# Decoding the chosen sub-keys and experts of a routed feed-forward layer for four heads at once

## The chip, the cores and the metric

One core of one Trainium2 chip runs one program on inputs that lie in HBM. The metric is the device time in microseconds (us), lower is better. The kernel before took 3133.07 us (median of 3 runs, 3132.15 to 3140.36).

## The reference, cut to what matters

The program is a stack of transformer blocks over 512 tokens of width 1024: two blocks with a dense feed-forward part, then one block whose feed-forward part is a product-key expert layer. The change lies in that layer's routing:

```
q = (x_blk @ w_query).reshape(b, t, PEER_HEADS, 2, HALF_KEY)
scores = jnp.einsum('bthcd,hcnd->bthcn', q, sub_keys)
top_s, top_i = lax.top_k(scores, PEER_TOPK)
cand_s = top_s[..., 0, :, None] + top_s[..., 1, None, :]
cand_i = top_i[..., 0, :, None] * N_KEYS + top_i[..., 1, None, :]
...
best_s, pos = lax.top_k(cand_s, PEER_TOPK)
expert_idx = jnp.take_along_axis(cand_i, pos, axis=-1)
```

There are 8 heads, 128 keys in each half, and 16 kept of each top-k. So each token and head has 16 x 16 candidates, of which 16 positions are kept. A position 0 to 255 says which of the 16 kept keys of the first half (position shifted right by 4) and which of the second half (position and 15) were taken; decoding looks up the numbers of those two keys.

## The kernel before, in words

The work runs on five engines, each with its own queue: TensorE (PE) for products, VectorE (DVE), ScalarE (ACT), GpSimd (POOL), and SyncE (SP), which issues most DMAs. All products are made in three passes over operands that are split in a high and a low part. `split` (line 227) writes the high part on ACT (L228) and the low part on DVE or POOL (L229); `load_w` loads weights of 128x1024 and splits each half so. `LO` says which engine makes the low part: both halves on POOL during the first token half, one on POOL and one on DVE during the second.

The expert layer treats the 512 tokens as two halves of 256 (`PA` and `PB`, two objects of the class `Peer`), each of two tiles of 128 tokens (`NT` = 2). `queries` (line 1429) makes the query of a head with PE, copies it with ACT (L1439), and then calls `route` (line 1449) for the head before. For each of the two tiles `route` scores the keys with PE (L1456), copies the scores to `sc` with ACT (L1459), of which there are two buffers, and then works on DVE alone:

- `top16` (L1465 to L1469) twice over 128 scores and once over the 256 sums `cand` (L1477): five instructions each, max, index, replace, max, index.
- the decode, once per head and tile: `tf` (L1475) turns the key numbers into floats; for each half c, `ai` (L1485) cuts the position, `af` (L1488) turns it into a float, `oh` (L1490) compares it with 0 to 15, `oh` (L1492) multiplies by the key numbers, and a sum along 16 (L1493) writes the number to `i1` or `i2`. For the first tile of the first half (`ng` = 1), two more, `xi` (L1497) and `ix` (L1498), make the number of the expert's row.

So a head and tile have 11 decode instructions, 13 where `xi` and `ix` are made. The 256-wide ones are three in each half.

The generators are woven together by `alongside`: each has a number of steps, and at every turn the one that is least far along goes next. During `PA.queries` the last dense feed-forward part (`ffn_b`) goes along, during `PB.queries` the scores of all experts for three of the four tiles (`scores`, products of 128x384) and the gathered rows of the fourth (`gather_a`: an indirect DMA on POOL, L1503, and one 128x1024 multiply and sum on DVE, L1517). A scheduler then orders the instructions of each engine from this program order and a timing model of its own; every engine runs its queue in order. After `PB.queries` come the one-hot tables (`spread`, L1550 to L1564) and the sums over all experts (`experts`, L1614 to L1670), whose accumulators stay in PSUM throughout; the change has no line there.

Of the kernel before, what the change touches and what calls it, by code (L numbers as in the profile page):

```python
# [9 lines left out]
F = mybir.dt.float32  # L10
FR = mybir.dt.float32r
I32 = mybir.dt.int32
U32 = mybir.dt.uint32
I8 = mybir.dt.int8
AF = mybir.ActivationFunctionType
OP = mybir.AluOpType
AX = mybir.AxisListType
# [35 lines left out]
F_1, F_2, F_3, F_4, L_4 = 1, 36, 2, 20, 1  # L53
L_A = 0.01
S_1, S_2, G_1, G_2, G_3 = 20, 40, 60, 80, 260
# [114 lines left out]
def alongside(main, *others):  # L170

    live = [[g, n, 0] for g, n in (main,) + others]
    while True:
        e = min(live, key=lambda e: e[2] / e[1])
        e[2] += 1
        try:
            next(e[0])
        except StopIteration:
            if e[0] is main[0]:
                return  # L180
            live.remove(e)
# [7 lines left out]
def build(tc, A, out, stop=None, dump=None):  # L189
    nc = tc.nc  # L190
    V, SC, PE, GP = nc.vector, nc.scalar, nc.tensor, nc.gpsimd
    ctx = ExitStack()
    with ctx:
# [8 lines left out]
        def ps(w=S):  # L202
            t = psum.tile([128, S], F, name="ps")
            return t[:, :w] if w < S else t
# [131 lines left out]
        class Norm:  # L336


            def __init__(self, x, gcol, xh, xl, w=S, acc=None, sq=None, R=None):
                self.x, self.g, self.xh, self.xl, self.w = x, gcol, xh, xl, w  # L340
                self.done, self.squared = 0, 0
                self.acc = tmp.tile([128, w], F, name="sqa", bufs=1) if acc is None else acc
                self.r = tmp.tile([128, 4], F, name="rcol", bufs=4)[:, :w // 128]
                self.R = tmp.tile([128, w], F, name="R") if R is None else R
                self.sq = sq
# [204 lines left out]
        with tc.tile_pool(name="l0", bufs=1) as lp:  # L550
# [97 lines left out]
            for g in range(4):  # L648
# [6 lines left out]
                b = 8 + n // 2 - 1  # L655
# [87 lines left out]
        with tc.tile_pool(name="l1", bufs=1) as lp:  # L743
# [24 lines left out]
            p = ps()  # L768
# [186 lines left out]
        ffn_b = ffn1(W)  # L955
# [416 lines left out]
        iota = pe.tile([128, 128], F, name="iota")  # L1372
# [6 lines left out]
        RP = {}  # L1379
# [28 lines left out]
        class Peer:  # L1408
            def __init__(self, h, xh, xl, pool, ng):
                self.xh, self.xl, self.ng = xh, xl, ng  # L1410
                self.q0, self.t0, self.sl = h.q0, h.t0, h.sl
                self.h2 = [hp.tile([128, D], F, name="h2", bufs=ng) for _ in range(ng)]
                self.sd = [pe.tile([128, 8, 16], F, name="sd", bufs=ng) for _ in range(ng)]
                self.ix = [pe.tile([128, 8, 16], I32, name="ix", bufs=ng) for _ in range(ng)]
                self.bs, self.i1, self.i2 = ([pool.tile([128, 8, 16], F, name=n, bufs=2) for _ in range(NT)]
                                             for n in ("bs", "i1", "i2"))
                self.idx = {}

            def rows(self, t):

# [28 lines left out]
            def route(self, hd, qh):  # L1449
                rp = RP[0]  # L1450
                keysT = rp.tile([128, 2, 128], F, name="keysT", bufs=2)
                nc.sync.dma_start(keysT, A["keysT"][:, 2 * hd:2 * hd + 2])
                for t in range(NT):
                    p = ps(W)
                    for c in range(2):
                        PE.matmul(p[:, c * 128:(c + 1) * 128], qh[:, c, t * 128:(t + 1) * 128], keysT[:, c],  # L1456
                                  start=True, stop=True)
                    sc = rp.tile([128, 256], F, name="sc", bufs=2)
                    SC.activation(sc, p, AF.Copy)  # L1459
                    yield  # L1460
                    ts = rp.tile([128, 2, 16], F, name="ts", bufs=2)
                    ti = rp.tile([128, 2, 16], U32, name="ti", bufs=2)

                    def top16(vals, idx, src):
                        V.max(vals[:, 0:8], src)  # L1465
                        V.max_index(idx[:, 0:8], vals[:, 0:8], src)
                        V.match_replace(src, vals[:, 0:8], src, LOWEST)
                        V.max(vals[:, 8:16], src)
                        V.max_index(idx[:, 8:16], vals[:, 8:16], src)  # L1469

                    for c in range(2):
                        top16(ts[:, c], ti[:, c], sc[:, c * 128:(c + 1) * 128])
                        yield
                    tf = rp.tile([128, 2, 16], F, name="tf", bufs=2)
                    V.tensor_copy(tf, ti)  # L1475
                    cand = rp.tile([128, 256], F, name="cand", bufs=2)
                    V.tensor_add(cand.rearrange("p (a b) -> p a b", a=16), ts[:, 0][:, :, None].to_broadcast([128, 16, 16]),  # L1477
                                 ts[:, 1][:, None, :].to_broadcast([128, 16, 16]))
                    bp = rp.tile([128, 16], U32, name="bp", bufs=2)
                    top16(self.bs[t][:, hd], bp, cand)  # L1480
                    yield
                    x = (self.i1[t][:, hd], self.i2[t][:, hd])
                    for c in range(2):
                        ai = rp.tile([128, 16], I32, name="ai", bufs=2)
                        V.tensor_scalar(ai, bp.bitcast(I32), (4, 15)[c], None,  # L1485
                                        op0=(OP.logical_shift_right, OP.bitwise_and)[c])
                        af = rp.tile([128, 16], F, name="af", bufs=2)
                        V.tensor_copy(af, ai)  # L1488
                        oh = rp.tile([128, 16, 16], F, name="oh", bufs=2)
                        V.tensor_tensor(oh, af[:, :, None].to_broadcast([128, 16, 16]),  # L1490
                                        iota[:, None, :16].to_broadcast([128, 16, 16]), op=OP.is_equal)
                        V.tensor_mul(oh, oh, tf[:, c][:, None, :].to_broadcast([128, 16, 16]))  # L1492
                        V.reduce_sum(x[c], oh, axis=AX.X)  # L1493
                        yield
                    if t < self.ng:
                        xi = rp.tile([128, 16], F, name="xi", bufs=2)
                        V.scalar_tensor_tensor(xi, x[0], 128.0, x[1], op0=OP.mult, op1=OP.add)  # L1497
                        V.tensor_copy(self.ix[t][:, hd], xi)  # L1498
                        self.idx[t, hd] = self.ix[t][:, hd]

            def gather(self, table, t, hd, j):
# [197 lines left out]
        PA = Peer(HA, xh, xl, pe, NG)  # L1699
# [7 lines left out]
        gather_a = gathered()  # L1707

        alongside((normed(0, W, xh, xl), 20), (ffn_b, F_3))
        alongside((PA.queries(), 140), (ffn_b, F_4), (gather_a, L_4))  # L1710
        low(LO_Z)
        for _ in ffn_b:
            pass
# [20 lines left out]
        PB = Peer(HB, yh[:, :, rest], yl[:, :, rest], dp, 0)  # L1734
# [13 lines left out]
                    yield from p.one_hots(t)  # L1748

        scores_ = scores(yh, yl)  # L1750
        alongside((PB.queries(), 114), (scores_, S_1), (gather_a, G_1))
        alongside((spread(), 69 * NV), (scores_, S_2), (gather_a, G_2))
        for _ in scores_:
            pass
# [35 lines left out]
```

## Time and profile before

| | us |
|---|---|
| median of 3 runs | 3133.07 |
| the profiled execution, its own time | 3134.13 |
| its span in the trace | 3132.4 |
| outside the span | 1.7 |
| PE busy | 2938.3 (94%) |
| DVE busy | 2207.6 (70%) |
| ACT busy | 1372.6 (44%) |
| POOL busy | 1147.2 (37%) |

Busy time is summed over the whole span. The chain that ended last is 71% PE and 21% DVE. Which engine sets the pace is another one in each stage, so the shares of the whole say little of a change to the routing; the routing of the first token half lies at about 1424 to 1632 us from the start, that of the second at about 1880 to 2164 us.

### The profile page before, as it was taken

The numbers are of one execution on the slowest core, as the hardware profiler recorded it, in microseconds if no ns is written. First come the engines' busy times: TensorE is split into PE (matmuls) and PEld (weight loads), VectorE is DVE, ScalarE is ACT, GpSimd is POOL, SyncE is SP. The second block draws the span as 40 slices with busy tenths as digits, with TensorE's granted clock in tenths as the row PEclk, the third lists the DMA queues.
The fourth block names the chain that finished last, engine by engine and source line by source line (L and its number), as shares of the span: only waits on it lengthen the run. The fifth ranks groups of instructions, "written<-read, shape, count | busy, mean of one in ns | idle before, by whom it ended". The sixth has DMA issues, their size and how long they took to land.

```text
span 3132.4 us, 44864 instructions
## 1 busy us (share of the span) xinstructions
PE 2938.3 (94%) x16770; PEld 2551.2 (81%) x16770; DVE 2207.6 (70%) x4148; ACT 1372.6 (44%) x2347; POOL 1147.2 (37%) x723
## 2 busy tenths in 40 slices
PE   8999999999989889998779989889999999999999
PEld 6468888867689888888769588888999998777787
DVE  6755434477766747658996569999787758888753
ACT  4443222466554545453244543336666653333333
POOL 3110000343320376466554235555554535445200
PEclk9999999999999989999889989999999999999999
DMA  3022232311145533234334038777788779999964
GB/s 132 25 67 101 88 101 88 107 54 48 35 158 194 175 132 125 87 132 142 118 112 151 1 121 281 254 274 256 275 316 305 283 286 383 382 380 370 338 229 151
DMA packets 195883, 568.30 MB, mean 181 GB/s; under 512 B 16944, under 2 KB 68528, under 8 KB 194000
## 3 DMA queue, kind: packets, MB, share of 16 engines
q1 hardware_dynamic: 157664, 427.61, 39.4%
q0 software_dynamic: 37712, 137.71, 11.9%
q8 instruction: 132, 2.16, 0.3%
q14 instruction: 87, 0.71, 0.1%
q10 hardware_dynamic: 288, 0.11, 0.0%
HBM read 512.93 MB, written 52.43 MB: 180 GB/s over the span
## 4 chain that ended last, share of the span: by engine, by line
PE 71%; DVE 21%; DMA 3%; issue 2%; ACT 2%; POOL 0%; DVEq 0%; SPq 0%; ACTq 0%; POOLq 0%
PE ps L266 15%; PE ps L267 15%; PE ps L268 15%; PE ps L1669 4%; PE ps L1670 4%; PE ps L1668 4%; PE ps L1550 2%; DVE u L1517 2%; DVE wlo L229 2%; PE ps L482 2%; DMA raw<-in_peer_v_dram 1%; PE ps L475 1%; DVE oh L1490 1%; PE ps L283 1%; PE ps L285 1%
## 5 line engine op out<-in xcount | busy, mean ns | idle before, releaser
L229 POOL TENSOR_TENSOR wlo<-raw,whi 128x1024 fp32r<-128x1024 f32 (+2 forms) x241 | 589.8, 2455 | 634.8 <-ACT whi L228 585.9
L228 ACT ACTIVATE whi<-raw 128x1024 fp32r<-128x1024 f32 (+2 forms) x518 | 516.2, 999 | 648.6 <-PE ps L267 391.8
L229 DVE TENSOR_TENSOR wlo<-raw,whi 128x1024 fp32r<-128x1024 f32 (+3 forms) x277 | 334.0, 1207 | 215.3 <-ACT whi L228 214.6
L268 PE MATMUL ps<-yh,wlo 128*128 128x384 f32 (+1 forms) x1152 | 387.5, 337 | 27.7 <-DVE wlo L229 27.6
L266 PE MATMUL ps<-yh,whi 128*128 128x384 f32 (+1 forms) x1152 | 389.9, 339 | 0.0
L267 PE MATMUL ps<-yl,whi 128*128 128x384 f32 (+1 forms) x1152 | 385.1, 334 | 0.0
L1669 PE MATMUL ps<-vl,gh 128*128 128x512 f32 x768 | 301.1, 392 | 4.2 <-DVE vl L229 4.1
L1670 PE MATMUL ps<-vh,gl 128*128 128x512 f32 x768 | 299.9, 391 | 0.0
L266 PE MATMUL ps<-XH,whi 128*128 128x512 f32 (+1 forms) x680 | 273.2, 406 | 8.7 <-ACT whi L228 8.7
L1503 POOL DMA_INDIRECT u<-in_peer_v_dram,ix x128 | 197.5, 1543 | 197.8 <-DVE h L1582 182.5
L267 PE MATMUL ps<-XL,whi 128*128 128x512 f32 (+1 forms) x680 | 267.7, 396 | 0.0
L268 PE MATMUL ps<-XH,wlo 128*128 128x512 f32 (+1 forms) x680 | 263.1, 395 | 1.3 <-DVE wlo L229 1.3
L1668 PE MATMUL ps<-vh,gh 128*128 128x512 f32 x768 | 239.8, 392 | 9.2 <-ACT vh L228 9.2
L268 PEld LDWEIGHTS ps<-yh,wlo 128*128 128x128 f32 x1152 | 220.4, 191 | 32.4 <-DVE wlo L229 32.4
L228 ACT ACTIVATE vh<-raw 128x1024 fp32r<-128x1024 f32 x128 | 133.5, 1056 | 253.9 <-DMA raw<-in_peer_v_dram 183.4
L266 PE MATMUL ps<-fx,whi 128*128 128x256 f32 x704 | 202.6, 292 | 26.0 <-ACT whi L228 21.4
L1517 DVE SCALAR_TENSOR_TENSOR u<-u,h 128x1024 f32<-128x1024 f32 x127 | 203.1, 1604 | 32.4 <-DMA u<-in_peer_u_dram,ix 32.2
L266 PEld LDWEIGHTS ps<-yh,whi 128*128 128x128 f32 x1152 | 220.9, 192 | 0.0
L267 PEld LDWEIGHTS ps<-yl,whi 128*128 128x128 f32 x1152 | 220.5, 191 | 0.0
L366 POOL TENSOR_TENSOR sqa<-sqa,sq 128x512 f32<-128x512 f32 (+1 forms) x28 | 42.1, 1505 | 450.5 <-ACT sq L364 449.6
L229 DVE TENSOR_TENSOR vl<-raw,vh 128x1024 fp32r<-128x1024 f32 x128 | 155.5, 1221 | 65.7 <-ACT vh L228 65.0
L267 PE MATMUL ps<-fx,whi 128*128 128x256 f32 x704 | 199.6, 287 | 0.9 <-DVE fx L351 0.9
(427 smaller groups left out, 7244.4 us busy)
## 6 DMA issues: line engine op xcount, KB each, us to landing
raw<-in_uT_dram SPq DMA_DIRECT2D x128, 512.0 KB
raw<-in_peer_v_dram SPq DMA_DIRECT2D x128, 512.0 KB
raw<-in_w_gate_dram SPq DMA_DIRECT2D x66, 512.0 KB
raw<-in_w_up_dram SPq DMA_DIRECT2D x66, 512.0 KB
raw<-in_w_in_dram SPq DMA_DIRECT2D x52, 512.0 KB
Sd<-s SPq DMA_DIRECT2D x32, 768.0 KB
Gd<-st SPq DMA_DIRECT2D x12, 2048.0 KB
gt<-Gd SPq DMA_DIRECT2D x32, 768.0 KB
```

What stands on the lines that cost most here:

```text
L228: SC.activation(hi, src, AF.Copy)
L229: eng.tensor_sub(lo, src, hi.bitcast(F))
L266: PE.matmul(out, wh, xh, start=first, stop=False)
L267: PE.matmul(out, wh, xl, start=False, stop=False)
L268: PE.matmul(out, wl, xh, start=False, stop=last)
L482: PE.matmul(po[hd], vtile(hd, j), t[hd, j], start=j == 0, stop=j == nk - 1)
L1503: i = GP.indirect_dma_start(out=u, out_offset=None, in_=A[table], in_offset=bass.IndirectOffsetOnAxis(ap=self.idx[t, hd][:, j:j + 1], axis=0))
L1517: V.scalar_tensor_tensor(u, u, 1.0, self.h2[t], op0=OP.mult, op1=OP.mult, accum_out=self.sd[t][:, hd, j:j + 1])
L1550: PE.matmul(p[:, n * 128:(n + 1) * 128], q[:, n], e[:, n], start=True, stop=True)
L1668: PE.matmul(p, gh[:, e, ts], h[:, cs], start=False, stop=False, skip_group_check=True)
L1669: PE.matmul(p, gh[:, e, ts], l[:, cs], start=False, stop=False, skip_group_check=True)
L1670: PE.matmul(p, gl[:, e, ts], h[:, cs], start=False, stop=end, skip_group_check=True)
```

## The change

The decode moves out of `route` into a new function `decode`, which is called after every fourth head for four heads of a tile. The tiles `ti` and `bp` hold four heads. Each decode instruction stays, with four times the elements: the 256-wide ones become 1024-wide, `ai` and `af` 64-wide, `tf` 128-wide. The scratch tiles of the decode have one buffer instead of two; `oh` has four times the size. The numbers that `alongside` takes for the steps of `queries` follow (140 to 112, 114 to 91), since `queries` has fewer steps.

```diff
@@ route, class Peer
+                    h4 = hd % 4
+                    if h4 == 0:
+                        self.ti[t] = rp.tile([128, 4, 2, 16], U32, name="ti", bufs=2)
+                        self.bp[t] = rp.tile([128, 4, 16], U32, name="bp", bufs=2)
                     ts = rp.tile([128, 2, 16], F, name="ts", bufs=2)
-                    ti = rp.tile([128, 2, 16], U32, name="ti", bufs=2)
+                    ti, bp = self.ti[t][:, h4], self.bp[t][:, h4]
...
-                    tf = rp.tile([128, 2, 16], F, name="tf", bufs=2)
-                    V.tensor_copy(tf, ti)
...
-                    bp = rp.tile([128, 16], U32, name="bp", bufs=2)
                     top16(self.bs[t][:, hd], bp, cand)
                     yield
-                    x = (self.i1[t][:, hd], self.i2[t][:, hd])
-                    for c in range(2):
...
-                        V.reduce_sum(x[c], oh, axis=AX.X)
-                        yield
...
+                    if h4 == 3:
+                        yield from self.decode(t, hd - 3)
+
+            def decode(self, t, h0):
+
+                rp = RP[0]
+                hs = slice(h0, h0 + 4)
+                tf = rp.tile([128, 4, 2, 16], F, name="tf", bufs=1)
+                V.tensor_copy(tf, self.ti[t])
+                x = (self.i1[t][:, hs], self.i2[t][:, hs])
+                full = [128, 4, 16, 16]
+                for c in range(2):
+                    ai = rp.tile([128, 4, 16], I32, name="ai", bufs=1)
+                    V.tensor_scalar(ai, self.bp[t].bitcast(I32), (4, 15)[c], None,
+                                    op0=(OP.logical_shift_right, OP.bitwise_and)[c])
+                    af = rp.tile([128, 4, 16], F, name="af", bufs=1)
+                    V.tensor_copy(af, ai)
+                    oh = rp.tile(full, F, name="oh", bufs=1)
+                    V.tensor_tensor(oh.rearrange("p h a b -> p (h a) b"),
+                                    af.rearrange("p h a -> p (h a)")[:, :, None].to_broadcast([128, 64, 16]),
+                                    iota[:, None, :16].to_broadcast([128, 64, 16]), op=OP.is_equal)
+                    V.tensor_mul(oh, oh, tf[:, :, c][:, :, None, :].to_broadcast(full))
+                    V.reduce_sum(x[c], oh, axis=AX.X)
+                    yield
+                if t < self.ng:
+                    xi = rp.tile([128, 4, 16], F, name="xi", bufs=1)
+                    V.scalar_tensor_tensor(xi, x[0], 128.0, x[1], op0=OP.mult, op1=OP.add)
+                    V.tensor_copy(self.ix[t][:, hs], xi)
+                    for hd in range(h0, h0 + 4):
                         self.idx[t, hd] = self.ix[t][:, hd]
@@ the stages
-        alongside((PA.queries(), 140), (ffn_b, F_4), (gather_a, L_4))
+        alongside((PA.queries(), 112), (ffn_b, F_4), (gather_a, L_4))
-        alongside((PB.queries(), 114), (scores_, S_1), (gather_a, G_1))
+        alongside((PB.queries(), 91), (scores_, S_1), (gather_a, G_1))
```

Two places of DVE's queue show what moves. The first is in the routing of the first token half: before, in the middle of it (the names are those of the text above; `MAX` to `MATCH_REPLACE` are `top16`):

```order
L1490 TENSOR_TENSOR oh<-af,iota 128x256
L1497 SCALAR_TENSOR_TENSOR xi<-i_12649,i_12651 128x16
L1490 TENSOR_TENSOR oh<-af,iota 128x256
L1467 MATCH_REPLACE cand<-bs,cand 128x256
L1468 MAX bs<-cand 128x8
L1492 TENSOR_TENSOR oh<-oh,tf 128x256
L1498 CAST ix<-xi 128x16
L1492 TENSOR_TENSOR oh<-oh,tf 128x256
L1468 MAX bs<-cand 128x8
L1469 MAX_INDEX bp<-bs,cand 128x8
```

and with the change, after the fourth head (the lines of `top16` are now L1469 to L1473, those of the decode L1491 to L1510; L541 adds a result of `ffn_b` to the activations):

```order
L1501 TENSOR_TENSOR oh<-af,iota 128x1024
L1496 TENSOR_SCALAR ai<-bp 128x64
L1471 MATCH_REPLACE cand<-bs,cand 128x256
L1504 TENSOR_TENSOR oh<-oh,tf 128x1024
L1499 CAST af<-ai 128x64
L1472 MAX bs<-cand 128x8
L1505 TENSOR_REDUCE i_12649<-oh 128x64
L1473 MAX_INDEX bp<-bs,cand 128x8
L1501 TENSOR_TENSOR oh<-af,iota 128x1024
L1496 TENSOR_SCALAR ai<-bp 128x64
```

The decode is gone from between the searches of the other heads, and stands, longer, at two places in each token half.

The second is in the routing of the second token half, where low parts of weights (`wlo`, L229), which PE needs, and sums of gathered rows (`u`, L1517, with the change L1530) stand in the same queue. Before:

```order
L229 TENSOR_TENSOR wlo<-raw,whi 128x1024
L1492 TENSOR_TENSOR oh<-oh,tf 128x256 x2
L1485 TENSOR_SCALAR ai<-bp 128x16 x2
L1493 TENSOR_REDUCE i_17397<-oh 128x16
L1493 TENSOR_REDUCE i_17399<-oh 128x16
L1488 CAST af<-ai 128x16 x2
L1517 SCALAR_TENSOR_TENSOR u,sd<-u,h_12644 128x1024
L1490 TENSOR_TENSOR oh<-af,iota 128x256 x2
L1517 SCALAR_TENSOR_TENSOR u,sd<-u,h_12644 128x1024
L1492 TENSOR_TENSOR oh<-oh,tf 128x256
L229 TENSOR_TENSOR wlo<-raw,whi 128x1024
```

With the change, after the fourth head:

```order
L229 TENSOR_TENSOR wlo<-raw,whi 128x1024
L1505 TENSOR_REDUCE i_17139<-oh 128x64
L1471 MATCH_REPLACE cand<-bs,cand 128x256
L1530 SCALAR_TENSOR_TENSOR u,sd<-u,h_12644 128x1024
L1501 TENSOR_TENSOR oh<-af,iota 128x1024
L1472 MAX bs<-cand 128x8
L1530 SCALAR_TENSOR_TENSOR u,sd<-u,h_12644 128x1024
L1504 TENSOR_TENSOR oh<-oh,tf 128x1024
L1473 MAX_INDEX bp<-bs,cand 128x8
L229 TENSOR_TENSOR wlo<-raw,whi 128x1024
```

Between two low parts there now stand three decode instructions of 1024 elements, where seven of 256 and four short ones stood.

## Rows read from the trace of the kernel before

**Rows 1.** Windows: busy us (count) of PE, PEld, DVE, ACT, POOL; PE clock; DMA share, GB/s
```profile
1424.00:1632.00 208.00, 155.38 (x1136) 148.25 (x1135) 206.54 (x654) 70.35 (x116) 111.31 (x56) 0.88 0.35 118
1880.00:2164.00 284.00, 253.23 (x1516) 247.89 (x1515) 282.31 (x750) 105.38 (x180) 158.17 (x92) 0.97 0.75 260
2164.00:2560.00 396.00, 393.27 (x2497) 392.85 (x2496) 307.88 (x356) 257.74 (x596) 195.54 (x108) 1.00 0.81 295
```

**Rows 2.** Chain of waits by line, 1424 to 1632 us
```profile
by line: DVE af L1488 9.3%; DVE oh L1490 7.9%; DVE cand L1477 6.5%; DVE ai L1485 5.1%; DVE oh L1492 4.6%; DVE ti L1466 4.1%; DVE i L1493 4.1%; DVE sc L1467 4.1%; DVE ti L1469 3.8%; DVE wlo L229 3.4%; DVE q L516 3.2%; DVE xl L977 3.1%; DVE t
```

**Rows 3.** Chain of waits by line, 1880 to 2164 us
```profile
by line: DVE u L1517 25.4%; DVE wlo L229 15.1%; DVE oh L1492 5.2%; DVE oh L1490 4.2%; DVE cand L1477 3.8%; issue 3.4%; DMA u<-in_peer_u_dram,ix 2.9%; DVE i L1493 2.8%; DVE ti L1469 2.8%; DVE ti L1466 2.7%; PE ps L268 2.7%; DVE sc L1467 2.6%
```

**Rows 4.** Who waited for whom, 1424 to 1632 us: total us, times, longest
```profile
ACT sc L1459 <- DVE ti L1469: 34.7, 7, 14.7
PE ps L266 <- ACT whi L228: 31.3, 9, 9.7
```

**Rows 5.** The same, 1880 to 2164 us
```profile
PE ps L268 <- DVE wlo L229: 27.6, 15, 4.7
```

**Rows 6.** Timeline of DVE: start us, us
```profile
1562.12 0.16 DVE L1485 TENSOR_SCALAR ai<-bp 128x16 int32<-128x16 int32 x1
1562.20 0.41 DVE L1490 TENSOR_TENSOR oh<-af,iota 128x256 f32<-128x256 f32 x1
1562.53 0.16 DVE L1485 TENSOR_SCALAR ai<-bp 128x16 int32<-128x16 int32 x1
...
1566.34 2.37 DVE L1488 CAST af<-ai 128x16 f32<-128x16 int32 x1
```

**Rows 7.** Chain of waits in order of time: start us, us, what
```profile
1930.29 1.12 DVE wlo L229
```

**Rows 8.** DVE, 1424 to 1640 us, by form: count, busy us, mean ns, idle before
```profile
L1488 DVE CAST af<-ai 128x16 f32<-128x16 int32 x32 | 21.2, 699 | 0.0
L1490 DVE TENSOR_TENSOR oh<-af,iota 128x256 f32<-128x256 f32 x32 | 19.8, 639 | 0.0
L1477 DVE TENSOR_TENSOR cand<-ts 128x256 f32<-128x256 f32 x16 | 15.1, 947 | 0.0
L1492 DVE TENSOR_TENSOR oh<-oh,tf 128x256 f32<-128x256 f32 x32 | 14.2, 465 | 0.0
L1485 DVE TENSOR_SCALAR ai<-bp 128x16 int32<-128x16 int32 x32 | 12.3, 421 | 0.0
L1493 DVE TENSOR_REDUCE i<-oh 128x16 f32<-128x256 f32 x32 | 12.0, 404 | 0.0
...
L1497 DVE SCALAR_TENSOR_TENSOR xi<-i,i 128x16 f32<-128x16 f32 x8 | 6.7, 840 | 0.0
...
L1475 DVE CAST tf<-ti 128x32 f32<-128x32 uint32 x16 | 6.0, 375 | 0.0
L1498 DVE CAST ix<-xi 128x16 int32<-128x16 f32 x8 | 5.9, 736 | 0.0
```

**Rows 9.** Timeline of POOL at the same place
```profile
1563.34 5.34 POOL L229 TENSOR_TENSOR wlo<-raw,whi 128x1024 fp32r<-128x1024 f32 x2 [6.84 <-ACT whi L228]
```

**Rows 10.** DVE, 1880 to 2172 us, by form
```profile
L229 DVE TENSOR_TENSOR wlo<-raw,whi 128x1024 fp32r<-128x1024 f32 x30 | 48.5, 1615 | 0.0
L1492 DVE TENSOR_TENSOR oh<-oh,tf 128x256 f32<-128x256 f32 x32 | 18.8, 621 | 0.0
L1490 DVE TENSOR_TENSOR oh<-af,iota 128x256 f32<-128x256 f32 x32 | 16.0, 535 | 0.0
L1477 DVE TENSOR_TENSOR cand<-ts 128x256 f32<-128x256 f32 x16 | 12.5, 780 | 0.0
...
L1485 DVE TENSOR_SCALAR ai<-bp 128x16 int32<-128x16 int32 x32 | 9.9, 365 | 0.1
L1488 DVE CAST af<-ai 128x16 f32<-128x16 int32 x32 | 6.5, 265 | 0.0
...
L1475 DVE CAST tf<-ti 128x32 f32<-128x32 uint32 x16 | 4.8, 299 | 0.0
```

More of the change, by code (lines that the diff above doesn't have):

```diff
@@ L1416, in __init__ @@
                                              for n in ("bs", "i1", "i2"))
-                self.idx = {}
+                self.idx, self.ti, self.bp = {}, {}, {}
             def rows(self, t):
@@ L1478, in route @@
                                  ts[:, 1][:, None, :].to_broadcast([128, 16, 16]))
-                    bp = rp.tile([128, 16], U32, name="bp", bufs=2)
                     top16(self.bs[t][:, hd], bp, cand)
                     yield
-                    x = (self.i1[t][:, hd], self.i2[t][:, hd])
-                    for c in range(2):
[L1484 to L1492, printed above, removed]
-                        V.reduce_sum(x[c], oh, axis=AX.X)
-                        yield
@@ L1495, in route @@
[L1495 to L1498, printed above, removed]
+                    if h4 == 3:
[25 more added lines that the diff above has]
+                    for hd in range(h0, h0 + 4):
```

## The prediction

> **What bounds the kernel now.** I read the windows first, with their cuts at the two stretches in which the decode runs [rows 1]. From 1424 to 1632 us DVE is busy 206.5 of 208 us, PE 155.4; from 1880 to 2164 us DVE 282.3 of 284, PE 253.2. Right behind, from 2164 us, PE is busy 393.3 of 396 and DVE 308. So DVE sets the pace just where the change cuts its work, and PE sets it afterwards: what the two stretches lose in length should stay lost. In the first PE idles 52.6 us and its granted clock is 0.88, in the second it idles 30.8 at 0.97. The chain says the same by line: in the first stretch nearly all its named lines are DVE's, with the decode's `af`, `oh` (twice), `ai` and sum at 9.3 + 7.9 + 4.6 + 5.1 + 4.1 = 31% [rows 2]; in the second the two `oh` and the sum have 12%, behind the gathered rows and the low parts of weights [rows 3]. The waits tell how PE hangs on it. In the first stretch PE waits 31.3 us for high parts from ACT, whose queue stands 34.7 us at the copy to `sc` until a DVE search frees a buffer [rows 4]; in the second PE waits 27.6 us for low parts that stand in DVE's queue [rows 5].
>
> **What the decode costs now.** Two things must be kept apart, DVE's work and its waits. DVE starts the next instruction before the last one's recorded end: 0.08 us after a 16-wide one, 0.33 us after a 256-wide one [rows 6], though they are recorded with 0.16 and 0.41; a 1024-wide low part takes 1.12 us of the chain [rows 7]. Four of 256 take 1.32, one of 1024 takes 1.12, so an instruction costs (1.32 - 1.12) / 3 = 0.066 us beside its elements. The elements are the same before and after.
>
> The waits: a short instruction that stands nowhere is recorded with 0.16 us [rows 6], but `af` has a mean of 0.699 in the first stretch [rows 8]. The cast at 1566.34 took 2.37 us, and POOL was then in two splits that took 5.34 us together from 1563.34 on [rows 6, 9]: DVE stood until POOL was through. The sums never do this (0.404 us, mean of 32 [rows 8]). I therefore count as wait all that lies above 0.404 for 256 elements and above 0.16 for the short ones. First stretch [rows 8]: `af` 21.2 - 5.1 = 16.1, comparison 19.8 - 12.9 = 6.9, product 14.2 - 12.9 = 1.3, `ai` 12.3 - 5.1 = 7.2, `xi` and `ix` 12.6 - 2.6 = 10.0, `tf` 6.0 - 2.6 = 3.4: 44.9 us. Second [rows 10], in the same way: product 5.9, comparison 3.1, `ai` 4.8, `af` 1.4, `tf` 2.2: 17.4 us.
>
> **The change, part by part.** *Fewer instructions.* A head and tile have 11 now, two more where `xi` and `ix` are made. First stretch: 16 x 11 + 16 = 192 before, 4 x 11 + 4 = 48 after, 144 fewer, x 0.066 = 9.5 us. Second: 176 before, 44 after, 132 fewer, 8.7 us. The Trainium skill, VectorE: DVE Perf Modes, in its section on the TRN2 errata, has a larger price: VectorE reading SBUF pays a fixed latency per instruction, which it measured as about 150 cycles at 0.96 GHz. By that, 0.156 us, an estimate from the page, this term would be 22 and 21 us, and the time some 18 us lower than forecast below; the starts in the timeline here do not show it, since instructions overlap by about that much, and the sum goes by the starts.
>
> *Fewer waits.* The trace does not show how long a decode of four heads waits. From above: as long in all as now, because POOL has the same splits to make (nothing gained, and a loss is excluded by there being fewer DVE instructions that can meet them). From below: a quarter, as many as there are instructions left. Between them I take the row that already stands alone between searches, as the new ones will: `cand`, once per head and tile, waits 0.947 - 0.404 = 0.54 us in the first stretch and 0.780 - 0.404 = 0.38 in the second [rows 8, 10]. Without the 8 sums, 40 and 36 instructions are left that can wait: 21.7 and 13.5 us. Gained: 23.2 and 3.9 us; bounds 0 to 33.7 and 0 to 13.1.
>
> So DVE loses 32.7 us of work and waits in the first stretch and 12.6 in the second (bounds 9.5 to 43.2 and 8.7 to 21.8).
>
> *Work in lumps.* The decode now comes at the fourth and eighth head. First stretch: the new decode is 192 - 144 = 48 instructions of about 30 us in all (24 x 1.12, and 24 short ones at 0.08 to 0.15) and 21.7 us of waits, 13 us per tile and call; the rest of DVE's 208 - 33 = 175 us, 123, is 7.7 per head and tile, against PE's 155.4 / 16 = 9.7. Without a decode PE is the slower one, with it DVE. If PE could not run ahead, the stretch would take 12 x 9.7 + 4 x 20.7 = 199 us, 9 less than now; if it runs ahead freely, 175. It can run ahead by the two `sc` buffers, some 19 us, against 2 x (20.7 - 9.7) = 22 of lag: most of it. Second stretch: the decode is 10.8 per call, the rest 14.3 per head and tile, PE 253.2 / 16 = 15.8. Without running ahead 12 x 15.8 + 4 x 25.1 = 290, 6 us longer than now; freely 271. Here PE needs a low part from DVE every 253 / 30 = 8.4 us [rows 10], and in the new order the place shown between two of them holds five long instructions (three of the decode, two gathered rows) and three searches, 5 x 1.12 + 3 x 0.33 = 6.6 us without waits: the low parts need not come late. I take three quarters of DVE's gain in both: 24.5 and 9.5 us.
>
> *Moved and unchanged.* The indices of gathered rows, `ix`, come for four heads at a time, later for the first three; but the weaving gives the gathers one step against all 140 (now 112) of this stage, so no gather waits for them. `i1` and `i2` of the last four heads come at the stage's very end; the one-hot tables begin with a tile of the first token half, whose numbers are long there. The single buffers of the scratch tiles are written and read by DVE alone, in order: nothing. The step counts 112 and 91 follow the fewer steps, so `ffn_b`, scores and gathers go along at the same share. No DMA is added.
>
> **Sum.** 3134.1 (the profiled execution, 3132.4 of it span) - 24.5 - 9.5 = 3100.1; its distance to the median of the runs is 1.1, so the median should be **3099 us**.
>
> **The rivals.** *A, the waits belong to POOL.* DVE stands about once for each POOL split, at the next instruction of its own that collides, whichever it is. Then a fourfold shorter list of decode instructions meets the same splits, `cand`, the residual sums and the gathered rows take over the waits, and only the 18.2 us of fewer instructions are gained, three quarters of it 14: 3119. For it: many `af` wait whole splits; against it: searches and sums do not wait, and they are now longer among themselves. The Trainium skill, SBUF: State Buffer, section "Who interferes with whom", speaks for it: the read and write ports that VectorE shares with GpSimd go to whichever instruction began first, for its whole length, so a split blocks any colliding VectorE instruction, and a 1024-wide one holds POOL back longer than a 256-wide one did. The trace agrees in the one cast of 2.37 us. POOL has 97 us of idle time in the first stretch [rows 1], so what it waits more is hidden.
>
> *B, the lumps stop PE.* No running ahead: 9 us gained in the first stretch, 6 lost in the second, 3131, within 0.3%. For it: two `sc` buffers, and low parts in DVE's own queue; against it: the new order mixes searches and low parts into the decode.
>
> *C, slower: the lumps cost the clock.* As B, and PE, standing behind each lump in the second stretch, falls from a granted clock of 0.97 to the 0.88 that it has in the first, where it already stands in turns [rows 1]: 253 x (0.97 / 0.88 - 1) = 26 us more, 3134 - 9 + 6 + 26 = 3157. It decides once PE stands more than it does now, above 31 us of idle time in the second stretch; against it speaks that DVE has less to do there in all.
>
> **How the numbers follow.** Forecast 0.69, A 0.17, B 0.09, C 0.05. A measurement of this kernel can tell about 0.3%, 9.4 us, from no change. The low end is the lower bound of all waits with PE running freely ahead: 43.2 + 21.8 = 65, 3069. The high end takes in A with half of its 18 us used, 3124. Outside lie B, C and a little of the tails. Faster by over 0.3%: the forecast and most of A, 0.83; within 0.3%: B and the rest, 0.12; slower: 0.05.
>
> **What would show it.** In the changed trace: 4 `tf` of 128 per token half, 8 comparisons of 1024 with means near 1.2 us plus a wait; DVE's decode some 52 us in the first stretch; the first stretch about 24 us shorter and the second about 9, with PE's idle time there down by as much and its wait for low parts below 27.6; the stage behind 2164 as long as now. I am wrong if `cand` and the residual sums take over the waits (A), if PE's waits gather at the fourth and eighth head (B), or if the granted clock of the second stretch is lower (C); and if the later stages give back what the two gained.

## The result, and the profile after

The changed kernel takes 3093.0 us (median of 4 runs, 3089.7 to 3100.1) against 3136.7 for the kernel before in the same comparison: a ratio of 0.9864, 95% interval 0.9839 to 0.9889, some 44 us or 1.4% faster. Its profiled execution took 3092.1 us with a span of 3090.4, 42.0 less than the span before.

Where the 42 us lie is read from landmarks that both kernels have: the first key product of the first routing, the one gather that is issued behind that routing, the first gather beside the second routing, and the first product of the one-hot tables. The rows are those of single lines (ns min/median/max, first and last start in us), here of the kernel before:

```profile
L1456 PE MATMUL ps<-keysT,qh x128: 270/275/421, 1422.5 to 2102.8; 128*128 128x128 f32 x128
L1503 POOL DMA_INDIRECT q<-in_peer_u_dram,ix x1: 1037/1037/1037, 1632.6 to 1632.6; - x1
L1503 POOL DMA_INDIRECT u<-in_peer_u_dram,ix x127: 942/1231/1948, 1856.9 to 2465.0; - x127
L1550 PE MATMUL ps<-oe,oq x768: 270/275/377, 2124.1 to 2546.0; 128*128 128x128 f32 x192
```

and of the changed kernel:

```profile
L1456 PE MATMUL ps<-keysT,qh x128: 270/275/275, 1422.0 to 2058.9; 128*128 128x128 f32 x128
L1516 POOL DMA_INDIRECT q<-in_peer_u_dram,ix x1: 1037/1037/1037, 1593.4 to 1593.4; - x1
L1516 POOL DMA_INDIRECT u<-in_peer_u_dram,ix x127: 942/1235/1972, 1813.6 to 2424.1; - x127
L1563 PE MATMUL ps<-oe,oq x768: 270/275/377, 2082.3 to 2503.3; 128*128 128x128 f32 x192
```

Up to the first key product both are alike. From there to the first gather 210.1 us became 171.4: **38.7 us**. From there to the first gather of the second half 224.3 became 220.2: 4.1 us. From there to the first one-hot product, the second routing, 267.2 became 268.7: **nothing**. Behind it 1008.3 became 1008.1. So nearly all of the gain is in the first routing. The traces of the runs below say the same: from the first key product to the gather behind the first routing, three kernels whose first routing decodes head by head (the one before, e2, e9) take 206.8 to 210.1 us, and eight that decode four heads there 170.1 to 171.9.

The windows of the changed kernel, with the columns of [rows 1]: the first routing, the second (as long as in [rows 1]), and the stage of the one-hot tables. By these landmarks the windows of the second routing, here and in [rows 1], begin some 23 us behind the first gather and end 40 us behind the first one-hot product, and the last decode instructions run beside the one-hot tables (to 2171 us before, to 2131 with the change).

```profile
1424.00:1593.00 169.00, 142.06 (x1132) 138.04 (x1130) 166.31 (x512) 70.59 (x115) 113.85 (x55) 0.95 0.44 146
1838.00:2122.00 284.00, 255.27 (x1523) 250.43 (x1522) 268.52 (x622) 108.38 (x182) 166.32 (x93) 0.96 0.74 262
2122.00:2518.00 396.00, 394.10 (x2492) 392.77 (x2491) 308.15 (x348) 253.83 (x593) 195.55 (x108) 1.00 0.81 295
```

In the first routing DVE is 40.2 us less busy than in [rows 1] and still full; PE idles 26.9 us instead of 52.6, at a granted clock of 0.95 instead of 0.88. In the second DVE is 13.8 us less busy, but PE gets no more done: 255.3 against 253.2 us in 284.

What waited there, first in the first routing, answering to [rows 4]:

```profile
ACT sc L1459 <- DVE ti L1473: 20.9, 3, 14.0
...
PE ps L266 <- ACT whi L228: 9.6, 4, 7.6
```

then in the second, answering to [rows 5]:

```profile
PE ps L268 <- DVE wlo L229: 28.7, 17, 3.6
...
DVE u L1530 <- DMA u<-in_peer_u_dram,ix: 12.8, 6, 6.7
```

In the first routing ACT's copies and with them PE's high parts thus wait less; in the second PE waits for low parts as long as before (27.6), and DVE itself now stands 12.8 us for gathered rows that have not landed, where it stood 2.8.

DVE by form in the first routing (1424 to 1600 us; count, busy us, mean ns, idle before), answering to [rows 8]:

```profile
L1479 DVE TENSOR_TENSOR cand<-ts 128x256 f32<-128x256 f32 x16 | 18.3, 1147 | 0.0
L1501 DVE TENSOR_TENSOR oh<-af,iota 128x1024 f32<-128x1024 f32 x8 | 13.1, 1642 | 0.0
L1504 DVE TENSOR_TENSOR oh<-oh,tf 128x1024 f32<-128x1024 f32 x8 | 11.5, 1436 | 0.0
L1499 DVE CAST af<-ai 128x64 f32<-128x64 int32 x8 | 10.0, 1250 | 0.0
L1505 DVE TENSOR_REDUCE i<-oh 128x64 f32<-128x1024 f32 x8 | 9.6, 1203 | 0.0
...
L1496 DVE TENSOR_SCALAR ai<-bp 128x64 int32<-128x64 int32 x8 | 4.8, 599 | 0.0
...
L1510 DVE CAST ix<-xi 128x64 int32<-128x64 f32 x2 | 2.5, 1262 | 0.0
```

and in the second (1838 to 2131 us), answering to [rows 10]:

```profile
L1530 DVE SCALAR_TENSOR_TENSOR u<-u,h 128x1024 f32<-128x1024 f32 x66 | 94.3, 1432 | 12.8 <-DMA u<-in_peer_u_dram,ix 12.8
L229 DVE TENSOR_TENSOR wlo<-raw,whi 128x1024 fp32r<-128x1024 f32 x30 | 58.6, 1952 | 0.2 <-ACT whi L228 0.2
L1479 DVE TENSOR_TENSOR cand<-ts 128x256 f32<-128x256 f32 x16 | 14.7, 916 | 0.0
L1501 DVE TENSOR_TENSOR oh<-af,iota 128x1024 f32<-128x1024 f32 x8 | 11.9, 1484 | 0.0
L1504 DVE TENSOR_TENSOR oh<-oh,tf 128x1024 f32<-128x1024 f32 x8 | 9.7, 1210 | 0.0
...
L1574 DVE TENSOR_TENSOR oe<-iota,T 128x512 f32<-128x512 f32 x11 | 9.6, 875 | 0.0
```

with two more lines of the kernel before, in the window of [rows 10]:

```profile
L1517 DVE SCALAR_TENSOR_TENSOR u<-u,h 128x1024 f32<-128x1024 f32 x66 | 95.3, 1444 | 2.8 <-DMA u<-in_peer_u_dram,ix 2.8
...
L1561 DVE TENSOR_TENSOR oe<-iota,T 128x512 f32<-128x512 f32 x11 | 7.5, 682 | 0.0
```

With the sums (1.20 us, no wait) as the base of the 1024-wide ones, a bare 0.18 for `af` and `ai` and 0.16 for `ix`, the decode in the first routing waits 3.5 + 1.9 + 8.6 + 3.4 + 2.2 = 19.6 us, where it waited 44.9. `cand` took over 3.2 us of it.

In the second the decode is some 33 us shorter, and its waits fell from 17.4 us to some 2. There they passed to other instructions. I count as wait what lies above 1.20 us for a gathered row's sum or a low part, 0.40 for `cand` and 0.68 for the one-hot comparison `oe`. The low parts then waited 12.5 us before and 22.6 with the change, `cand` 6.1 and 8.3, `oe` 0 and 2.1, the sums of gathered rows 16.1 and 15.1. With the decode's own waits that is 52 us before and 50 with the change. The same count gives some 51 us in e1 and 49 in e2, which decode one head and four heads there. DVE's waits were not saved in the second routing, and the low parts, for which PE waits, took the most of them over.

A wait looks as it did, only rarer. DVE in the first routing of the changed kernel (start us, us):

```profile
1481.57 1.21 DVE L1504 TENSOR_TENSOR oh<-oh,tf 128x1024 f32<-128x1024 f32 x1
1482.70 2.39 DVE L1499 CAST af<-ai 128x64 f32<-128x64 int32 x1
1485.01 0.41 DVE L1472 MAX8 bs<-cand 128x8 f32<-128x256 f32 x1
```

and POOL beside it:

```profile
1482.11 5.28 POOL L229 TENSOR_TENSOR wlo<-raw,whi 128x1024 fp32r<-128x1024 f32 x2 [2.04 <-ACT whi L228]
```

The cast of 64 elements stands until the first of POOL's two splits is through; the search behind it then runs beside the second one.

### The profile page after: what moved, and what is told of

It reads as the page before. It is cut to its first block, busy times and chain, and to the rows that moved or that the text cites. A ratio compares the mean times of both kernels' runs of the same rounds, so it can differ in the third digit from the quotient of the medians.

```text
span 3090.4 us, 44585 instructions
## 1 busy us (share of the span) xinstructions
PE 2923.3 (95%) x16770; PEld 2539.4 (82%) x16770; DVE 2154.9 (70%) x3873; ACT 1370.7 (44%) x2347; POOL 1163.8 (38%) x722
## 4 chain that ended last, share of the span: by engine, by line
PE 71%; DVE 18%; DMA 5%; issue 3%; ACT 2%; POOL 1%; SPq 0%; DVEq 0%; ACTq 0%; POOLq 0%
PE ps L266 14%; PE ps L268 14%; PE ps L267 14%; PE ps L1682 4%; PE ps L1683 4%; PE ps L1681 4%; DVE wlo L229 2%; PE ps L1563 2%; DVE u L1530 2%; PE ps L482 2%; DMA u<-in_peer_v_dram,ix 1%; DMA u<-in_peer_u_dram,ix 1%; PE ps L475 1%; PE ps L283 1%; PE ps L285 1%
## 5 line engine op out<-in xcount | busy, mean ns | idle before, releaser
L229 POOL TENSOR_TENSOR wlo<-raw,whi 128x1024 fp32r<-128x1024 f32 (+2 forms) x240 | 595.7, 2490 | 584.8 <-ACT whi L228 571.0
L229 DVE TENSOR_TENSOR wlo<-raw,whi 128x1024 fp32r<-128x1024 f32 (+3 forms) x278 | 351.0, 1264 | 215.3 <-ACT whi L228 214.6
L1530 DVE SCALAR_TENSOR_TENSOR u<-u,h 128x1024 f32<-128x1024 f32 x127 | 190.1, 1502 | 49.3 <-DMA u<-in_peer_u_dram,ix 49.3
L266 PE MATMUL ps<-fx,whi 128*128 128x256 f32 x704 | 199.2, 287 | 4.5 <-ACT whi L228 3.1
L268 PE MATMUL ps<-fx,wlo 128*128 128x256 f32 x704 | 193.9, 284 | 6.9 <-DVE wlo L229 4.6
L229 DVE TENSOR_TENSOR vl<-raw,vh 128x1024 fp32r<-128x1024 f32 x128 | 155.0, 1221 | 63.2 <-ACT vh L228 62.7
```

The lines of the kernel that those rows point to most:

```text
L229: eng.tensor_sub(lo, src, hi.bitcast(F))
L266: PE.matmul(out, wh, xh, start=first, stop=False)
L268: PE.matmul(out, wl, xh, start=False, stop=last)
L1530: V.scalar_tensor_tensor(u, u, 1.0, self.h2[t], op0=OP.mult, op1=OP.mult, accum_out=self.sd[t][:, hd, j:j + 1])
```

## The experiments

Every ratio is against the kernel before, run beside the experiment on the same chip. It had 3138.8 us beside e1 to e4, 3138.2 beside e5 to e8 and 3139.6 beside e9 to e12.

**Each half alone, and the place without the size.** *e1* decodes four heads at once only in the first half; the second keeps its `route` of before, here called `route1`:

```diff
-                        yield from self.route(hd - 1, qs[hd - 1])
+                        yield from (self.route if self.ng else self.route1)(hd - 1, qs[hd - 1])
...
-        alongside((PB.queries(), 91), (scores_, S_1), (gather_a, G_1))
+        alongside((PB.queries(), 114), (scores_, S_1), (gather_a, G_1))
```

> Decode of four heads at once in the first token half only; the second half decodes head by head as before. Theory 1 (the whole gain is DVE time saved in the first routing, the second routing gained nothing): as the changed kernel, about 3093 us, routing of the first half about 39 us shorter than before, that of the second half 284 us long. Rival (the second routing did gain, and only the boundary between the stages hides it): 3100 to 3110.

3103.7 us, ratio 0.9891 (0.9871 to 0.9912). By the landmarks the routing of the first half took what it takes in the changed kernel (first gather at 1594.5), the second 272.1 us. The median lies in the rival's range and not at the 3093 of theory 1, but the interval overlaps that of the whole change, so the second half's part is small, if there is one.

*e2* is the reverse: four heads in the second half only (`route1 if self.ng else route`, step counts 140 and 91).

> Decode of four heads at once in the second token half only; the first half decodes head by head as before. Theory 1: no gain, 3133 to 3139 us, with DVE some 14 us less busy in the second routing and PE waiting as long for low parts as before (about 28 us). Rival: 10 to 15 us faster than before, 3122 to 3127.

3130.8 us, ratio 0.9975 (0.9961 to 0.9990): a quarter of a per cent, between the two expectations. Its profiled run shows none of it in the second routing, 266.6 us by the landmarks against 267.2 before; DVE was busy 242.8 of 266 us. The medians of e1 and e2 both leave some 8 to 10 us for the second half, and the landmarks of their single traces show none of it. Where these lie stays open; the first key product alone starts anywhere from 1422 to 1430 us in the traces of this case.

*e3* puts the decode after every fourth head, for four heads, but each instruction still takes one head (`decode1` is the decode of one head as it was, the step counts are those of before):

```diff
                     if h4 == 3:
-                        yield from self.decode(t, hd - 3)
+                        for h in range(4):
+                            tf = rp.tile([128, 2, 16], F, name="tf", bufs=2)
+                            V.tensor_copy(tf, self.ti[t][:, h])
+                            yield from self.decode1(t, hd - 3 + h, tf, self.bp[t][:, h])
```

> In both halves the decode stands after every fourth head, for four heads, but each instruction still takes one head (as many and as short as before). If fewer instructions and fewer waits made the gain: none of it, 3130 to 3145 us, DVE full for some 205 us in the first routing. If it is the place of the decode, in lumps away from the searches, that made it: 3093 to 3105.

3141.3 us, ratio 1.0004 (0.9991 to 1.0018), DVE busy 208.1 of 212 us in the first routing. Counted as in the prediction, the decode waits some 50 us there, no less than the 44.9 before. The place is worth nothing: it is that instructions are four times fewer.

**Waits or instructions?** *e7* and *e8* take POOL's splits out of the first routing, in the changed kernel and in the kernel before, by the same line; POOL keeps only its short additions there:

```diff
+        low(0)
         alongside((PA.queries(), 112), (ffn_b, F_4), (gather_a, L_4))
```

> As the changed kernel, with all low parts of weights made on DVE, none on POOL, while the first half is routed; beside e8, the same edit on the kernel before. If more than half of the gain in the first routing is waits for POOL's splits: with no splits there the decode of four heads gains only the 9.5 us of fewer instructions, so the first routing here is 8 to 16 us shorter than in e8, not 39. Each of the two is longer than its own base by up to 40 x 1.12 = 45 us of low parts less its waits: here 175 to 195 us (169 in the changed kernel).

> As the kernel before, with all low parts of weights made on DVE while the first half is routed. By the same theory the 45 us of waits in the decode vanish and 45 us of low parts come in: the first routing takes 190 to 210 us (208 before). If DVE's time there is its instructions and not waits: 235 to 250 us, and e7 some 39 us less.

3102.2 and 3113.2 us, one run each. The casts that stood behind POOL's splits (a mean of 699 ns before, 1250 with the change) no longer do, in e7

```profile
L1499 DVE CAST af<-ai 128x64 f32<-128x64 int32 x8 | 1.5, 183 | 0.0
```

nor in e8 (both 1424 to 1640 us):

```profile
L1488 DVE CAST af<-ai 128x16 f32<-128x16 int32 x32 | 6.6, 241 | 0.0
```

In all, the decode's waits there are 3 us in e7 (19.6 in the changed kernel) and 8 in e8 (44.9 before). So it was POOL's splits that the decode waited for. The landmarks are e7's

```profile
L1456 PE MATMUL ps<-keysT,qh x128: 270/275/275, 1422.9 to 2070.2; 128*128 128x128 f32 x128
L1516 POOL DMA_INDIRECT u<-in_peer_u_dram,ix x127: 942/1236/1977, 1824.1 to 2433.5; - x127
```

and e8's

```profile
L1456 PE MATMUL ps<-keysT,qh x128: 270/275/275, 1427.7 to 2079.4; 128*128 128x128 f32 x128
L1503 POOL DMA_INDIRECT u<-in_peer_u_dram,ix x127: 939/1180/1951, 1835.9 to 2444.5; - x127
```

From the first key product to the first gather of the second half, which takes in all that the low parts shifted, e8 takes 408.2 us and e7 401.2: with POOL's splits out of the way the decode of four heads is worth 7 us, and 11 in the whole time. With them in the way it is worth 434.4 - 391.6 = 42.8. So most of the 43 us hang on POOL's splits. The 7 are no clean price of the fewer instructions: the eight kernels with the new first routing spread over 8 us on this stretch (389.9 to 397.7), and by the last sum of the decode, 183.3 us after the first key product in e7 and 205.5 in e8, the two lie 22 us apart (174.9 and 211.2 with the splits). In e8 the next stage's first additions (L1104, from 1613.9 us) already stand ahead of that sum (1633.2).

And e8 alone, which does not touch the decode, gains 26 us on this stretch: DVE makes POOL's low parts, and even so it is through no later. In the changed kernel the same line loses: e7 is 10 us longer than it on the stretch, and 9 in all. The two remedies do not add up.

**What holds the second routing?** *e4* moves its decode behind it, next to the one-hot tables (the positions are kept in the pool of that stage, the step counts are 83 and 69 for each tile and 8 more):

```diff
                 for t in ts:
+                    if p is PB:
+                        yield from p.decode(t, 0)
+                        yield from p.decode(t, 4)
                     p.weights(t)
```

> As the changed kernel, but the second half's four decodes are made after its routing, next to the one-hot tables, where PE sets the pace and DVE has some 88 us to spare in 396. It takes about 35 us of DVE work and waits out of the second routing. If lumps of decode hold up the low parts there: the second routing shrinks by 10 to 25 us, 3068 to 3083 us in all. If the low parts wait for POOL's splits and for gathered rows that have not landed, lumps or not: the second routing stays within 8 us of 284, 3085 to 3093.

3110.1 us, ratio 0.9906 (0.9883 to 0.9929), slower than the changed kernel. The second routing takes 264.8 us by the landmarks, 4 less than in the changed kernel, in this window of it DVE is busy only 224.4 us (240.3 of 268 in the changed kernel), and PE has no more work done:

```profile
1823.00:2088.00 265.00, 238.74 (x1433) 234.60 (x1431) 224.41 (x562) 87.46 (x135) 156.59 (x90) 0.96 0.76 263
```

Its waits there:

```profile
DVE u L1536 <- DMA u<-in_peer_u_dram,ix: 28.0, 15, 5.4
PE ps L268 <- DVE wlo L229: 25.5, 12, 5.1
```

So it is hardly the decode, in lumps or at all, that holds the low parts: 16 us of DVE's time less shorten this stretch by 4, and DVE's waits for gathered rows grow to 28.0 us (18.7 on the same stretch of the changed kernel). The edit took out less than the 35 us that were meant: two of the decode's eight sums still stand in the stretch, and in the changed kernel only five do. The stage of the one-hot tables, from their first to their last product, grew from 421.0 to 432.5 us; its spare DVE time was not free.

*e5* gives the gathered rows six buffers instead of four (`UD` = 6).

> As the changed kernel, with six buffers for gathered rows instead of four from the second half's routing on. If gathered rows that have not landed hold up DVE's queue in the second routing: DVE's waits for them there (12.8 us in the changed kernel) nearly vanish and the stretch from the first gather to the first one-hot product falls from 268.7 to 250 to 260 us, 3075 to 3085 us in all. If what holds it is POOL's splits and the chain of weight loads and high parts: 265 to 272 us, 3088 to 3096.

3127.7 us, ratio 0.9964 (0.9951 to 0.9976): the second routing is 264.7 us long, so more buffers do not help there. They do not take away the waits for gathered rows either, 21.6 us on this stretch, so the edit does not test what it was to test. And the kernel is 35 us slower than the changed one. The loss is in the last stage: the 128 gathers of `peer_v` are issued in 389 us instead of 467,

```profile
L1516 POOL DMA_INDIRECT u<-in_peer_v_dram,ix x128: 939/1682/2302, 2430.3 to 2819.6; - x128
```

and beside them, in a stage whose DMA engines are full in both kernels (a share of 1.00 in the changed one), PE idles 33.6 us in 316, where it idled 10.7:

```profile
2504.00:2820.00 316.00, 282.44 (x1244) 232.72 (x1243) 258.75 (x201) 89.75 (x86) 180.62 (x119) 0.96 1.02 386
```

That the gathers crowd the loads of that stage is likely, but no run parts it.

*e6* weaves 2 steps of gathers instead of 60 into the second routing (`G_1` = 2); the others come behind it. *e9* does the same to the kernel before.

> As the changed kernel, with the gathers woven into the second routing cut from 60 to 2 (the others come in the stages behind it). Takes some 58 x 1.5 = 87 us of DVE, 58 x 1.3 = 75 us of POOL and all waits for landed rows out of the second routing. If gathers are what holds it: the stretch up to the first one-hot product falls from about 268 to 235 to 248 us, near PE's 239 of work, and what is gained may be lost behind it. If weight loads and high parts hold it: 260 to 270. The time in all: 3080 to 3120.

> As the kernel before, with the gathers woven into the second routing cut from 60 to 2, as e6 does to the changed kernel. If gathers alone hold the second routing and decode has room beside them: the stretch from the first gather to the first one-hot product is 229 to 238 us as in e6 (229), and the kernel is some 39 us slower than e6 by the first routing alone, 3105 to 3120. If the decode of four heads pays there once gathers are gone: 245 to 260 us.

3074.5 and 3102.1 us, one run each, both below what was expected; the second routing takes 229.3 and 225.7 us, and PE is all but full in e6 (its landmarks, then its window):

```profile
L1516 POOL DMA_INDIRECT u<-in_peer_u_dram,ix x127: 939/1417/2513, 1817.7 to 2636.0; - x127
L1563 PE MATMUL ps<-oe,oq x768: 270/275/377, 2047.0 to 2467.4; 128*128 128x128 f32 x192
...
1814.00:2057.00 243.00, 240.82 (x1515) 240.34 (x1515) 168.79 (x512) 102.15 (x164) 79.14 (x36) 0.99 0.51 173
```

Gathers are what holds it, and without them the decode of one head is no slower than that of four. Of the 39 us that e6 gains there, 18 are lost behind the last one-hot product (605.4 us from there to the end, 587.1 in the changed kernel), where the put-off gathers now stand.

*e10* keeps the gathers, but sums only the first 16 of the 1024 products of each row of `peer_u`, so the scores of the gathered tile are incomplete:

```diff
-                            V.scalar_tensor_tensor(u, u, 1.0, self.h2[t], op0=OP.mult, op1=OP.mult,
+                            V.scalar_tensor_tensor(u[:, :16], u[:, :16], 1.0, self.h2[t][:, :16], op0=OP.mult, op1=OP.mult,
```

> As the changed kernel, with the sum of each gathered row of peer_u over its first 16 of 1024 numbers only (the scores of the gathered tile are left incomplete); the gathers themselves, their issue on POOL and their DMAs stay. Takes some 60 x 1.05 = 63 us of DVE out of the second routing. If it is DVE's sums that hold it: its stretch falls from 268 to 230 to 245 us. If it is POOL, where gathers and low parts of weights stand in one queue and take turns with DVE's instructions: 255 to 268 us.

The second routing takes 233.1 us (3056.9 in all, one run), though DVE stands longer for rows than ever, 40.3 us, and POOL still issues as many gathers, 63 (landmarks, then the window):

```profile
L1516 POOL DMA_INDIRECT u<-in_peer_u_dram,ix x127: 942/963/1871, 1816.2 to 2382.3; - x127
L1563 PE MATMUL ps<-oe,oq x768: 270/275/275, 2049.3 to 2465.8; 128*128 128x128 f32 x192
...
1817.00:2050.00 233.00, 228.10 (x1438) 226.91 (x1437) 174.63 (x606) 95.07 (x142) 137.69 (x91) 1.00 0.85 301
```

So of a gather it is the 1024-wide sum on DVE, or what goes along with it, that costs PE its low parts, not the number of issues on POOL or the landing. It is not shown why 16 us less of DVE's time (e4) bring 4 and some 66 us less (e10) bring 36. The short sums also give a buffer back sooner, and they leave POOL and DVE fewer long instructions to stand behind: a gather's issue takes a mean of 1.10 us on POOL instead of 1.33, a low part on DVE 1.29 instead of 1.95. These go together here, and no run parts them.

**A version that beats both.** *e11* is e6 again, timed; *e12* gives the stage of the one-hot tables 112 gather steps instead of 80:

```diff
-S_1, S_2, G_1, G_2, G_3 = 20, 40, 60, 80, 260
+S_1, S_2, G_1, G_2, G_3 = 20, 40, 2, 112, 260
```

> The kernel of e6 again, timed against the kernel before, as a candidate that beats both: 3070 to 3082 us, 1.7 to 2.2% faster than before.

> As e11, with 112 steps of gathers instead of 80 given to the stage of the one-hot tables, so that fewer are left for the last stage, whose loads fill the DMA engines. If that stage has room (DVE 344 of 453 us in e6): 3060 to 3072 us. If its DVE or POOL then holds up the low parts as in the second routing: slower than e11, 3080 to 3100.

e11: 3075.1 us, ratio 0.9792 (0.9776 to 0.9809). e12: 3071.4 us, ratio 0.9777 (0.9761 to 0.9794), the fastest of those that compute everything, though its interval overlaps e11's. Two numbers that weave the gathers add some 24 us to the 44 of the change (68.1 us under the kernel before, in its own comparison).

## Why the prediction was right, and where its terms were not

The total was forecast at 34 us of gain, and 42 were found in the profiled run. That it came so near is in part luck: the first routing gained 14 us more than its 24.5 and the second nothing of its 9.5, two misses that partly cancel.

- *DVE sets the pace in both routings.* Right for the first. For the second only half: DVE was full, but PE hung on one kind of DVE instruction, the low parts, and what delays those is the gathered rows' sums in the same queue, with what goes along with them (e6, e10). A full engine on the chain did not mean that less of any of its work would help.
- *Fewer instructions, 9.5 us in the first routing.* The starts on which the price rests came out: a 1024-wide product that does not stand is followed after 1.13 us in the changed trace (1481.57 to 1482.70), with 1.12 taken. The term itself no run isolates, since what e7 gains on e8 is 7, 11 or 22 us, as one measures it. By the latency of 150 cycles per instruction that the Trainium skill gives (VectorE: DVE Perf Modes, the section on the TRN2 errata) it would have been 22. The same section's table has 58 cycles beside the elements, from which it would be 8.7, an estimate from the page; with these the starts of 0.08, 0.33 and 1.12 us here agree.
- *Fewer waits, 23.2 us in the first routing, 3.9 in the second.* In the first the decode's waits fell by 25, from 44.9 to 19.6, with 21.7 forecast as left. In the second the term failed: the decode lost 15 us of waits, more than forecast, and nearly all of them, 13, came back at other instructions, 10 at the low parts.
- *Rival A, the waits belong to POOL's splits and pass to the next instruction.* It has the right cause: without splits the waits and most of the gain are gone (e7, e8), as the rule on the shared port in the Trainium skill (SBUF: State Buffer, "Who interferes with whom") would have it. Its ending is right in the second routing and wrong in the first. There only `cand` took over a part, 3.2 us, and other waits fell too: the products of L516 went from 7.4 to 3.7 us, those of L977 from 9.3 to 6.4 (the same view of the two kernels). A likely reason, which no run tests, is what stands between the decode's instructions: mostly searches in the first routing, which do not wait (L1470 has a mean of 282 ns with the change, the same search 290 before), and sums and low parts in the second, which do.
- *Work in lumps, three quarters of DVE's gain in both routings.* This is the step that failed, both ways. In the first routing all of DVE's gain counted: it is 40.2 us less busy, and the stretch is 38.7 us shorter. DVE was never empty there, and PE's wait for high parts behind ACT's copies fell from 31.3 to 9.6. In the second none did, 9.5 forecast, about 0 found by the landmarks: DVE was 13.8 us less busy, and 10 of these are waits for gathered rows that had not landed. Whether the lumps themselves cost anything there is not settled: the second routing reads 267.2, 268.7, 272.1, 266.6 and 264.8 us in the kernel before, the changed one, e1, e2 and e4, and 275.1 in e3, which has lumps of short instructions.
- *Rivals B and C* did not occur; the first routing gained far more than B's 9 us, and in the second the granted clock was 0.96 (0.97 before) and PE idled 28.7 us (30.8 before).

## What to carry to other kernels

Where DVE and GpSimd both work on SBUF, count the DVE instructions that can stand behind a GpSimd instruction, not only their lengths: in the first routing four times fewer of them saved 25 us of their waits. Then look at what stands next in the queue, since in the second routing the waits only moved on to it. Moving the GpSimd work away is worth trying first, since it cost one line and gained 26 us alone; but on top of the shorter decode the same line lost 10. And when an engine is full in a stage, find which of its instructions the next engine waits for and what stands ahead of that one; work that stands elsewhere in the queue can go away without a gain.

## What was not expected of the hardware

Moving POOL's splits to DVE (e8) put 39 more low parts of 1024 elements, 47 us, into a full DVE's queue (1424 to 1640 us), and DVE was through no later: its last decode sum starts 205.5 us after the first key product, 207.8 to 211.2 in the kernels that leave the splits on POOL (before, e2, e9). A split took POOL 2.45 us and takes DVE 1.22, and what DVE lost by standing behind POOL made up for the rest: the decode's waits fell from 44.9 to 8 us and those of `cand` from 8.7 to 1.0.

In the second routing DVE's waits stayed at some 50 us in all, whether 144 decode instructions or 36 could stand behind POOL's splits. Two more buffers for gathered rows (e5) made the kernel 35 us slower: the gathers of `peer_v` are issued in 389 us instead of 467, and PE idles three times as long beside them.
